# Layer 0's state space preparation moved behind the first sweep of the tokens

## The chip, the cores and the metric

The kernel runs on one core of one Trainium2 chip. A core has five engines with an instruction queue each, which they take in order: PE (TensorE, matrix multiplications; PEld is its weight load), DVE (VectorE), ACT (ScalarE), POOL (GpSimd) and SP (SyncE, which here issues most DMAs). The metric is the device time of one execution in microseconds (us). Before the change it is 5153.67 us, the median of 3 runs (5150.55 to 5157.43).

## The reference, cut to what matters

Two layers work on 2048 latent and 256 context tokens of width 1024. Each layer modulates the tokens, projects them once, feeds four mixers (A: grouped-query attention, B: differential attention, C: neighbourhood attention, D: a state space layer), gates and projects out:

```python
shift, scale, gate = jnp.split(silu(c) @ w_ada + b_ada, 3, axis=-1)
h = x * (1.0 + scale[:, None]) + shift[:, None]
(aq, ak, av, ag, ..., du, dg) = jnp.split(h @ w_in, IN_SPLITS, axis=-1)
...
yd, yd_c = s5_mixer(du, duc, a_re, a_im, log_dt, b_re, b_im, c_re, c_im, d_skip, w_glu, need_ctx)
y = jnp.concatenate([ya * silu(ag), ..., yd * silu(dg)], axis=-1) @ w_out
x_new = layer_norm(DEEPNORM_ALPHA * x + gate[:, None] * y, ln_g, ln_b)
```

Mixer D first turns its parameters into the matrices of a recurrence, and then scans the tokens in both directions. The first three lines need no token; this is what the kernel calls its preparation:

```python
lam_bar = jnp.exp(lam * dt)
b_bar = ((lam_bar - 1.0) / lam)[..., None] * b
# in s5_scan
bu = jnp.einsum('gpc,blgc->blgp', b_bar, u)
_, h = lax.associative_scan(_ssm_combine, (a, bu), axis=1)
# readout
y = einsum('gcp,blgp->blgc', c_f, h_f).real + einsum('gcp,blgp->blgc', c_b, h_b).real + d_skip * u
z = gelu(y) @ w_glu
```

## The kernel before, in words

Tokens are 18 tiles of 128 (two of context, 16 latent). Products in the projections are made in three matmuls of a high and a low part (L377 to L379). What precedes the attention of layer 0 runs in one stage, and this is its order in the code of `run`:

- **Modulation vectors** (`ada`, L242 on PE): 64 matmuls against 16 loads of `w_ada`.
- **Preparation** (`s5_prep`, L1320 to L1508): some 110 small DVE operations on 128x16 numbers, then complex products with POOL's help (`cmul`), then a loop over 16 groups. A group makes two tables, E and Fm (DVE L1479, L1481, L1483, L1485, L1487; POOL L1480, L1482), transposes E (PE L1494), multiplies Fm (PE L1501, L1502), assembles kf (ACT; DVE L1506, L1507) and stores three matrices to DRAM: `binm`, `coutm` and `t0`.
- **First sweep** (`proj_d`): for each tile, load x (L394, 512 KB), modulate (DVE L325, ACT L328), split into high and low parts (ACT L334, POOL L336, DVE L337), store them (L398, 1024 KB), 24 matmuls of 256 columns, copy (ACT L1519), transpose (PE L1523), copy out (DVE L1527). Then 16 stores of u to DRAM (L1534).
- **Group D, first pass** (L1661): loads u and `binm`, 256 matmuls, copies into B.
- **Scan** (L1578 to L1580 on DVE; carries and their products on DVE and POOL, L1624 to L1627).
- **Second sweep** (`proj("a0", ...)` with `proj_dg`): gate of D and projection of unit a0, the first half of mixer A, tile by tile from the stored parts (POOL issues these loads, L388), with an epilogue on all engines (L546 to L635). Its weights are split on POOL (L363, L367).
- **Group D, second pass** (from L1678): per group matmuls with `t0`, u, `coutm` and the states (L1701 and L1703), a GELU on ACT and DVE, a store; **third part** (L1732 to L1738): 18 tiles through `w_glu`, the last operation of each on POOL, L1737.
- **Ahead** (`F.ahead`): the first matmuls of unit b0.

All of this goes to a scheduler that simulates the engines, takes the code's order as priority and writes each engine's queue; an instruction whose operands come later may let later code pass it. Tiles of SBUF come from pools; a pool that is opened where a closed one lay makes its tiles wait for the tiles that lay there. The pool of the first sweep's loads (`h0`), that of `ada` and that of the preparation (`s5`) share one place, and group D's pool comes to lie there after them. Behind this stage `chain` gives the attention out in an order written by hand on PE, DVE and ACT; it starts with unit a0's maxima (POOL L777, PE L787). Layer 1's preparation runs beside the output projection of layer 0 and isn't touched.

Of the kernel before, what the change touches and what calls it, by code (L numbers as in the profile page):

```python
# [158 lines left out]
class Net:  # L159
# [405 lines left out]
    def slot(self, nq):  # L565
# [6 lines left out]
        return tuple(self.ub.tile([128, k, 64], F32, name=n) for k, n in ((NT, "b_v"), (nq, "b_gt")))  # L572

    def proj_a(self, l, kv, run):
        nc, io = self.nc, self.io
        nq = NT if l == 0 else NLAT
# [12 lines left out]
        def epi(ts, ps):  # L589
# [34 lines left out]
            if full:  # L624
# [10 lines left out]
            nc.scalar.activation(k2[0:64, s], tr[0:64], AF.Copy)  # L635

        return U, run(l, [(128 * kv, 128), (256 + 64 * kv, 64), (512 + 128 * kv, 128), (384 + 64 * kv, 64)], (0, 384),
                      (128, 384), epi, begin)

    def proj_b(self, l, h, run):  # L640
        nc, io = self.nc, self.io
        nq = NT if l == 0 else NLAT
# [1243 lines left out]
    def run(self):  # L1886
        self.consts()
        self.binm, self.coutm, self.t0 = {}, {}, {}
        for l in range(DEPTH):
            with ExitStack() as es:  # L1890
                side = "right" if l else "left"
                self.wp = self.pool(es, "wp", side=side)
                self.hp = self.pool(es, "hp", side=side)
                self.ep = self.pool(es, "ep", bufs=2)
                self.ub = self.pool(es, "ub")
                self.vg = [None]
                U = {}
                self.b_consts(l)

                def auto(*others):  # L1900
                    def run(l, segs, cols, ctx_cols, epi, begin):
                        begin()
                        self.sweep(l, [*others, (segs, cols, ctx_cols, epi, None, self.nc.gpsimd)])
                    return run

                def proj(u, run):
                    f = {"a": self.proj_a, "b": self.proj_b, "c": self.proj_c}[u[0]]
                    U[u], r = f(l, int(u[1]), run)
                    return r

                self.ua = self.pool(es, "ua")
                beside = lambda u: lambda F, prev: proj(u, lambda *a: self.sweep_beside(prev, F, *a))
                chunks = [(l, 4), (l, 5)] + [(l + 1, c) for c in range(4) if l + 1 < DEPTH]
                F = Fill([(u, beside(u)) for u in UNITS[1:]]
                         + [("ada", lambda F, prev: self.ada_beside(prev, F, chunks))])
                self.nd = 3
                with self.stage():
                    if l == 0:
                        with ExitStack() as es1:
                            self.ada(0, self.pool(es1, "ad"))  # L1920
                            self.s5_prep(0)
                    self.proj_d(l)
                    d = self.group_d(l)
                    next(d)
                    next(d)
                    proj("a0", auto(self.proj_dg(l)))
                    next(d, None)
                    self.ps_k = self.ps_tr
                    F.ahead(UNITS[1], AHEAD)
                self.ap = self.pool(es, "ap", bufs=2)  # L1930
                self.chain(l, F, U)
            self.nd = 2
            with self.stage():
                self.out_proj(l)
# [69 lines left out]
```

## Time and profile before

| What | us |
|---|---|
| Median of 3 runs | 5153.67 |
| The profiled execution | 5158.76 |
| Its span in the profile | 5156.9 |
| PE busy | 4681.1 (91%) |
| DVE busy | 3215.5 (62%) |
| POOL busy | 1912.5 (37%) |
| Loads of w_ada (L238), 512 KB each | 48, 4.5 to land |
| Loads of x (L394), 512 KB each | 18, 6.6 to land |

The durations in the rows below are of the one profiled execution; times of a row count from the start of its span. In the stretches, busy time counts overlapping instructions once; a busy engine is not always the one that others wait for. What ended an idle time stands behind an arrow.

### The profile page before, as it was taken

How to read it: one execution, taken by the hardware profiler on the slowest of the kernel's cores; microseconds unless marked ns; L12 is line 12 of the kernel's file. 1: busy time of each engine (PE TensorE's matmuls, PEld its weight loads, DVE VectorE, ACT ScalarE, POOL GpSimd, SP SyncE). 2: the span in 40 equal slices, each digit the busy share in tenths (PEclk: the TensorE clock that was granted, in tenths of full speed). 3: DMA queues.
4: the chain of work that ended last, by engine and by line, in shares of the span. 5: the costliest groups of instructions: out<-in, count | busy, mean ns of one | idle time of the engine just before them, and what ended most of it. 6: DMA issues, size and time to landing. Idle time of an engine off the chain costs nothing. (4 is left out here: it accounts for less than half of the span.)

```text
span 5156.9 us, 85866 instructions
## 1 busy us (share of the span) xinstructions
PE 4681.1 (91%) x31076; PEld 3585.3 (70%) x31076; DVE 3215.5 (62%) x7061; ACT 2568.4 (50%) x6522; POOL 1912.5 (37%) x3035
## 2 busy tenths in 40 slices
PE   7788998899999999998996879988999999999998
PEld 3686646665678777776676866566657777877777
DVE  8473767676674846724972737686767648476245
ACT  3332346634675856744341233466346658566431
POOL 4363443434233233321642534434342332333112
PEclk8899999999999999999998999999999999999999
DMA  7847212322235344253668573123223343433432
GB/s 255 287 151 202 88 41 66 98 95 72 91 121 167 103 144 132 83 178 116 194 213 281 169 198 109 49 65 98 95 72 98 111 152 100 155 122 117 130 134 107
DMA packets 360184, 677.66 MB, mean 131 GB/s; under 512 B 161872, under 2 KB 262224, under 8 KB 306768
## 3 DMA queue, kind: packets, MB, share of 16 engines
q0 software_dynamic: 54432, 396.39, 22.9%
q1 hardware_dynamic: 299280, 270.47, 17.9%
q10 hardware_dynamic: 6048, 5.31, 0.3%
q8 instruction: 247, 4.05, 0.3%
q14 instruction: 177, 1.45, 0.1%
HBM read 561.66 MB, written 110.36 MB: 130 GB/s over the span
## 5 line engine op out<-in xcount | busy, mean ns | idle before, releaser
L377 PE MATMUL pj<-WH,hs 128*128 128x256 f32 (+2 forms) x2592 | 814.9, 314 | 22.1 <-ACT b_v L733 7.1
L378 PE MATMUL pj<-WL,hs 128*128 128x256 f32 (+2 forms) x2592 | 753.3, 291 | 2.7 <-POOL WL L367 2.7
L379 PE MATMUL pj<-WH,hs 128*128 128x256 f32 (+2 forms) x2592 | 752.3, 290 | 0.0
L1114 ACT ACTIVATE PT<-tr 128x512 f32<-128x512 f32 (+1 forms) x788 | 440.5, 559 | 310.0 <-PE tr L1100 303.3
L377 PEld LDWEIGHTS pj<-WH,hs 128*128 128x128 f32 x2592 | 498.1, 192 | 125.3 <-issue 68.2
L388 POOL DMA_DIRECT2D hs<-hs x378 | 227.7, 603 | 956.0 <-PE pj L379 475.6
L378 PEld LDWEIGHTS pj<-WL,hs 128*128 128x128 f32 x2592 | 499.2, 193 | 26.6 <-POOL WL L367 3.3
L881 ACT ACTIVATE PT<-sx 128x512 f32<-128x512 f32 x584 | 315.3, 592 | 378.1 <-PE sx L879 367.6
L379 PEld LDWEIGHTS pj<-WH,hs 128*128 128x128 f32 x2592 | 497.7, 192 | 2.4 <-issue 2.4
L1045 DVE TENSOR_REDUCE sm<-sx 128x1 f32<-128x1024 f32 (+1 forms) x276 | 321.8, 1166 | 210.2 <-PE sx L1001 208.9
L1060 ACT ACTIVATE Ta<-sx,sm 128x1024 f32<-128x1024 f32 (+1 forms) x340 | 324.5, 955 | 108.2 <-DVE sm L1054 87.2
L886 PE MATMUL acc<-PT,a_v 128*64 128x512 f32 (+1 forms) x1168 | 315.8, 617 | 0.0
L897 POOL TENSOR_TENSOR Ta<-Ta,PT 128x512 f32<-128x512 f32 x160 | 219.5, 1389 | 204.4 <-ACT PT L881 203.9
L1126 PE MATMUL acc<-PT,b_v 128*64 128x128 f32 (+1 forms) x3200 | 277.9, 290 | 4.4 <-DVE sm L1073 1.5
L1001 PE MATMUL sx<-b_kst,qs 128*128 128x512 f32 (+2 forms) x618 | 218.3, 441 | 58.1 <-ACT Ta L1060 57.4
L814 DVE TENSOR_REDUCE mxa<-sy 128x1 f32<-128x1024 f32 (+1 forms) x256 | 209.8, 820 | 89.9 <-PE sy L812 86.8
L897 DVE TENSOR_TENSOR Ta<-Ta,PT 128x512 f32<-128x512 f32 x288 | 217.0, 794 | 77.0 <-ACT PT L881 76.5
L878 PE MATMUL sx<-Tb,a_kst 128*128 128x512 f32 x584 | 246.8, 423 | 19.5 <-ACT PT L881 19.5
L1100 PE MATMUL tr<-ident,Ta 128*128 128x128 f32 x1576 | 246.5, 278 | 13.9 <-ACT PT L1114 10.2
L1045 DVE TENSOR_REDUCE sm<-sy 128x1 f32<-128x768 f32 (+1 forms) x260 | 245.4, 944 | 15.7 <-PE sy L1001 14.4
L814 DVE TENSOR_REDUCE mxa<-sz 128x1 f32<-128x512 f32 x256 | 175.5, 686 | 123.5 <-PE sz L812 121.7
L377 PE MATMUL s<-WH,hs 128*128 128x256 f32 (+1 forms) x576 | 193.4, 337 | 44.9 <-DMA hs<-hs 20.7
(388 smaller groups left out, 12175.2 us busy)
## 6 DMA issues: line engine op xcount, KB each, us to landing
hs<-hs POOLq DMA_DIRECT2D x378, 1024.0 KB, 5.2
hs<-hs SPq DMA_DIRECT2D x36, 1024.0 KB, 4.8
hs<-in_w_ada SPq DMA_DIRECT2D x48, 512.0 KB, 4.5
wst<-in_w_in SPq DMA_DIRECT2D x576, 32.0 KB, 1.9
yin<-y SPq DMA_DIRECT2D x30, 512.0 KB, 4.0
h<-in_xT SPq DMA_DIRECT2D x18, 512.0 KB, 6.6
U<-ud SPq DMA_DIRECT2D x64, 144.0 KB, 3.6
x<-zn SPq DMA_DIRECT2D x18, 512.0 KB, 2.7
```

The costliest lines, as they stand in the source:

```text
L377: nc.tensor.matmul(ps, H[:, k, :], WH[k][:, c0:c1], start=(k == 0), stop=False)
L378: nc.tensor.matmul(ps, H[:, k, :], WL[k][:, c0:c1], start=False, stop=False)
L379: nc.tensor.matmul(ps, L[:, k, :], WH[k][:, c0:c1], start=False, stop=(k == NK - 1))
L814: nc.vector.tensor_reduce(nm if one else mx[:, j:j + 1], s, axis=AX.X, op=OP.max, negate=one)
L878: nc.tensor.matmul(o[:, h * 512:h * 512 + w], kst[:, ks], Q[0][:, h, :w], start=True, stop=False)
L881: nc.scalar.activation(PTs[x][h][:, :w], o[:, h * 512:h * 512 + w], AF.Exp, scale=0.125)
L886: nc.tensor.matmul(acc[h * 64:(h + 1) * 64, :w], v[:, kts[x], :], PT[h][:, :w], start=(x == 0), stop=(x == n - 1))
L897: eng.tensor_tensor(sums[e][:, h, :w], first[:, :w], PT[h][:, :w], op=OP.add)
L1045: nc.vector.tensor_reduce(mx[:, j:j + 1] if len(tiles) > 1 else nm, s, axis=AX.X, op=OP.max, negate=len(tiles) == 1)
L1060: nc.scalar.activation(r["P"](a, b), src, AF.Exp, bias=r["sm"][:, 5:6], accum_out=r["sm"][:, 6 + j:7 + j])
L1114: nc.scalar.activation(PT[:w, x:y], tr[:w, x * 128:y * 128].rearrange("p (a b) -> p a b", b=128), AF.Copy)
L1126: nc.tensor.matmul(acc[t][half * 64:half * 64 + 64, :], G["v"][:w, kt, :], PT[:w, j, :], start=(x < 2), stop=x >= nkt - 2)
```

## The change

The call `self.s5_prep(0)` moves from ahead of `self.proj_d(l)` to behind it. The code of the preparation is the same, and so is its work.

```diff
                     if l == 0:
                         with ExitStack() as es1:
                             self.ada(0, self.pool(es1, "ad"))
-                            self.s5_prep(0)
                     self.proj_d(l)
+                    if l == 0:
+                        self.s5_prep(0)
                     d = self.group_d(l)
```

With the call, the scheduler's queues change. On DVE, around the first tiles of the first sweep, the preparation (L1479 to L1507) and the modulation (L325) stood mixed before:

```order
L325 TENSOR_SCALAR h_1280<-h_1280,mod_78 128x128
L1507 TENSOR_TENSOR kf<-d,kf 16x16
L325 TENSOR_SCALAR h_1280<-h_1280,mod_78 128x128 x3
L1479 TENSOR_TENSOR m_763<-s_44_523,s_4_346 128x288
L1481 TENSOR_TENSOR m_765<-s_44_523,s_4_346 128x288
L1479 TENSOR_TENSOR m_796<-s_43_522,s_42_471 128x256
L1481 TENSOR_TENSOR m_798<-s_43_522,s_42_471 128x256
L1506 TENSOR_TENSOR kf<-d,s_45_534 16x16
```

At the same place there is now the sweep alone (L1527 copies its transposed result out):

```order
L325 TENSOR_SCALAR h_389<-h_389,mod_78 128x128 x4
L325 TENSOR_SCALAR h_431<-h_431,mod_78 128x128 x4
L337 TENSOR_TENSOR hs<-h_389,hs 128x768
L337 TENSOR_TENSOR hs<-h_431,hs 128x768
L325 TENSOR_SCALAR h_478<-h_478,mod_78 128x128 x4
L1527 COPY a_kst<-pj 128x16x8
L1527 COPY a_k_337<-pj 128x16x8
```

All 276 instructions of the preparation that stood ahead of or in the first sweep on DVE now stand behind its last split (L337). There they are mixed with the second sweep's epilogue (L546, L609, L627, L628 and others), here in the loop over the groups:

```order
L627 CAST ks<-kf 128x64
L546 SCALAR_TENSOR_TENSOR ks<-gth,s 128x256
L1507 TENSOR_TENSOR kf<-d,kf 16x16
L1483 TENSOR_TENSOR E<-m_1800,m_1801 128x256
L1487 TENSOR_TENSOR E<-m_1802,m_1803 128x256
L1479 TENSOR_TENSOR m_1810<-s_44_1441,s_4_1264 128x288
L1481 TENSOR_TENSOR m_1812<-s_44_1441,s_4_1264 128x288
L628 TENSOR_TENSOR ks<-kf,ks 128x64
```

Nine of the second sweep's 18 tiles have their epilogue (by L609) inside the preparation's queue; before, none had. On ACT, the copies L1678 that open group D's second pass stood among the second sweep's epilogue:

```order
L634 ACTIVATE a_kst<-pj 128x128
L635 ACTIVATE a_k_2928<-pj 64x128
L598 ACTIVATE pe<-s 128x320
L599 ACTIVATE a_v<-s 128x64
L1678 ACTIVATE big_2587<-big_2148 64x2304 x2
L602 ACTIVATE sq<-pe 128x192
```

Now the second sweep's epilogue ends before them, and the first tiles of unit b0 (L659, L660) stand between the scan's last carry (L1611) and the copies:

```order
L634 ACTIVATE a_kst<-pj 128x128
L635 ACTIVATE a_k_2928<-pj 64x128
L1611 ACTIVATE scan_c<-big_2429 128x2x16 x7
L659 ACTIVATE pe<-pj 128x2x64
L660 ACTIVATE pe<-pj 128x2x128
L537 ACTIVATE gth<-pe 128x128
L1678 ACTIVATE big_2587<-big_2148 64x2304 x2
```

What moved in between is the whole rest of the second sweep: it is done ahead of the copies now, where before it ran on behind them. POOL's last two products of the scan (L1626, L1627) stand behind a step of b0's epilogue (L541) in the same way.

## Rows read from the trace of the kernel before

**Rows 1.** Stretches: us, busy us (count) of PE, PEld, DVE, ACT, POOL; clock, DMA, GB/s.

```profile
62.00:155.00 93.00, 75.24 (x417) 51.76 (x416) 78.98 (x192) 45.06 (x104) 52.70 (x54) 0.85 0.88 286
155.00:207.00 52.00, 39.84 (x241) 37.02 (x241) 28.76 (x87) 23.75 (x48) 18.17 (x17) 0.80 0.84 294
207.00:272.00 65.00, 45.88 (x405) 42.18 (x406) 22.10 (x86) 16.98 (x51) 16.91 (x29) 0.87 0.83 248
272.00:363.00 91.00, 78.52 (x505) 76.87 (x504) 79.23 (x147) 25.40 (x93) 64.84 (x73) 0.92 0.44 142
363.00:437.00 74.00, 65.05 (x457) 62.26 (x456) 31.67 (x82) 32.17 (x66) 18.37 (x29) 0.98 0.81 213
437.00:491.00 54.00, 40.49 (x135) 21.57 (x133) 13.74 (x31) 9.36 (x30) 30.96 (x51) 0.89 0.64 180
```

**Rows 2.** Timeline: start us, us, engine, line, operation [idle before <-releaser].

```profile
490.18 0.72 POOL L1737 TENSOR_TENSOR yth<-yth,U 128x256 f32<-128x256 f32 x1 [0.60 <-DMA U<-dg]
...
490.98 2.33 POOL L777 TENSOR_TENSOR qn<-a_q,one 128x256 fp32r<-128x256 f32 x4
...
491.64 0.69 PE L787 MATMUL tr<-ident,qn 128*128 128x128 f32 x2 [6.90 <-POOL qn L777]
```

**Rows 3.** Four lines: ns min/median/max, first and last start us, forms.

```profile
L242 PE MATMUL pj<-hs,cs x64: 591/592/1057, 10.6 to 51.7; 128*2 128x512 f32 x64
L1507 DVE TENSOR_TENSOR kf<-d,kf x16: 152/155/163, 56.4 to 154.7; 16x16 f32<-16x16 f32 x16
L1519 ACT ACTIVATE ks<-s x18: 357/384/386, 77.4 to 201.5; 128x256 f32<-128x256 f32 x18
L1527 DVE COPY a_k<-pj x18: 269/279/282, 85.4 to 207.2; 128x128 f32<-128x128 f32 x18
```

**Rows 4.** Timeline of ACT, line 1519: two of eight such rows.

```profile
163.79 0.39 ACT L1519 ACTIVATE ks<-s 128x256 f32<-128x256 f32 x1 [2.88 <-PE s L379]
...
201.46 0.39 ACT L1519 ACTIVATE ks<-s 128x256 f32<-128x256 f32 x1 [3.11 <-PE s L379]
```

**Rows 5.** Waits from 155 to 205 us: engine, waited for, us, times, longest.

```profile
ACT h L328 <- DMA h<-in_xT: 8.9, 7, 2.6
```

**Rows 6.** Timeline, the preparation with no sweep beside it.

```profile
13.32 0.17 DVE L1420 TENSOR_TENSOR s<-s 128x16 f32<-128x16 f32 x1 [3.76 <-DMA s<-in_s_a]
...
28.39 0.42 DVE L1435 TENSOR_TENSOR cm<-s,s 128x256 f32<-128x256 f32 x1
...
43.50 0.88 PE L1494 MATMUL d<-ident,E 128*128 128x128 f32 x4
...
66.56 1.12 PE L1494 MATMUL d<-ident,E 128*128 128x128 f32 x4 [0.23 <-DVE kf L1507]
```

**Rows 7.** Groups by form, 13 to 62 us: busy us, mean ns, idle before.

```profile
L1479 DVE TENSOR_TENSOR m<-s,s 128x256 f32<-128x256 f32 x5 | 4.1, 814 | 0.0
```

**Rows 8.** Timeline of SP, POOL and PE behind the first sweep.

```profile
207.28 7.13 SPq L1534 DMA_DIRECT2D ud<-a_kst  x8
...
224.59 5.52 PE L1661 MATMUL d<-U,bm 128*64 128x144 f32 x48 [9.45 <-DMA U<-ud]
...
227.33 0.50 POOL L363 CAST WH<-wst 128x384 fp32r<-128x384 f32 x1 [22.76 <-DMA wst<-in_w_in]
```

**Rows 9.** Timeline of POOL in the scan, the first and last of its eight products.

```profile
322.20 2.40 POOL L1624 TENSOR_TENSOR big<-y,scan_c 128x1024 f32<-128x1024 f32 x1 [2.24 <-ACT scan_c L1611]
...
360.57 2.40 POOL L1627 TENSOR_TENSOR big<-big,big 128x1024 f32<-128x1024 f32 x1
```

**Rows 10.** Groups of DVE from 272 to 363 us: busy us, mean ns, idle.

```profile
L1580 DVE TENSOR_TENSOR big<-big 128x576 f32<-128x576 f32 (+1 forms) x24 | 17.4, 725 | 1.7 <-DVE big L1579 0.5
L1578 DVE TENSOR_TENSOR big<-coef,big 128x576 f32<-128x576 f32 x15 | 12.4, 829 | 0.4
L1579 DVE TENSOR_TENSOR big<-big,big 128x288 f32<-128x288 f32 x16 | 8.2, 514 | 0.2
```

**Rows 11.** DMA queues, 363 to 437 us: packets, MB, share of 16 engines (q0: L388).

```profile
q0 software_dynamic: 576, 4.19, 18.2%
```

## The prediction

> **What bounds the kernel now.** I read the stretches of layer 0 first, then backwards from the place where the attention starts. That place is the hand-over at 491 us: POOL ends the last L1737 of group D's third part, goes straight on to L777, the first operation of unit a0's maxima, and PE, idle for 6.9 us, is released by it [rows 2]. So the attention waits for the end of group D, and from there on the order is written by hand and the same in both kernels. What counts is how long it takes until group D is done. Its chain is a row of steps, and the stretches are cut where one ends [rows 1]: modulation vectors to 52.3 us (the last matmul of L242 starts at 51.7 and takes 0.6) [rows 3], first sweep to 207.5 (the last copy L1527 starts at 207.2), first pass to 272, scan to 363, second pass to 437, third part to 491.
>
> In which of these does the preparation cost anything? Its loop runs beside the sweep: L1507, once in a group, goes from 56.4 to 154.7 us [rows 3]. DVE is busy 79 of the 93 us of that stretch, and only 29 of the 52 behind it [rows 1]. The sweep itself went at (201.5 - 77.4)/17 = 7.3 us a tile over its whole length by L1519 [rows 3], but at (201.46 - 163.79)/7 = 5.38 us once the preparation had ended [rows 4]. There ACT waits for the loads of x [rows 5] while 294 GB/s move [rows 1]: a tile loads 512 KB and stores 1024, 1.57 MB, which at that rate takes 5.3 us. So that late pace is set by memory traffic, and the reader is to see two things: the preparation slows the sweep, and it is itself nearly free in the stretch ahead of 66 us and half free beside a sweep that waits for memory.
>
> **The change part by part.** Nothing is removed or added; the same instructions and DMAs run. The sum goes step by step along the chain to the hand-over, each with its value and both its ends.
>
> *First sweep, shorter.* Its modulation no longer queues behind the preparation. A load to its L1519 takes about two paces (two buffers of x), so the first one comes at 52.3 + 1.5 (copy, transpose, bias) + 2 x 5.4 = 64.6 instead of 77.4. Seventeen paces of 5.38 and 3 for the last transposes and copies: 64.6 + 91.5 + 3 = 159 us, against 207.5. Ends 153 and 165, since the stretches show 286 and 294 GB/s and no faster sweep. Gain 48 us.
>
> *The preparation's front, now on the path.* From its first operation to the first transposes it took 43.5 - 13.3 = 30.2 us with hardly anything beside it [rows 6]. Now POOL has ten splits of the second sweep's weights ahead of its first complex product, and these begin 20 us behind the first sweep (227.3 against 207.5), since their loads queue on SP behind the 16 stores of u that begin at 207.3 [rows 8]. I take 35, ends 30 and 42. The five loads of the preparation are issued on SP ahead of those stores, so they add nothing.
>
> *The loop over 16 groups.* With nothing beside it, four groups took 66.56 - 43.50 = 23.1 us, 5.8 each [rows 6]; beside the first sweep, (154.7 - 56.4)/15 = 6.55 each [rows 3]. The queue has nine tiles of the second sweep's epilogue in it, where the first sweep gave eleven or so, but each with six operations on POOL instead of one. I take 6.8: 109 us, ends 93 (5.8) and 128 (8.0). Its 48 stores and 192 matmuls ride along; PE does the second sweep's matmuls in between, and that cover holds.
>
> *First pass.* Before, it began 17 us behind the sweep, waiting for u (9.45 us on PE) [rows 8]. That wait falls away, as u is in DRAM long before. But `binm` of the last group must go to DRAM and back, and the pass then reloads u and `binm` through two buffers as before: 47 us as in 224.6 to 272; ends 38 (no waiting) and 65 (the whole stretch).
>
> *Scan.* Of 91 us, DVE's recurrence takes 17.4 + 12.4 + 8.2 = 38 [rows 10], and POOL's eight products of 2.4 us, 19, end at 363 [rows 9]; both ran mixed with the second sweep. About six of its tiles stay in the scan, none of them at its end, but there POOL now waits for b0's first two tiles before its last two products, and the copies L1678 queue on ACT behind the same tiles. I take 80; ends 57 (the two sums) and 91.
>
> *Second pass.* 74 us at 213 GB/s, DMA 81% busy [rows 1]: 15.8 MB, of which 4.2 are POOL's loads for the sweeps' tiles [rows 11], which don't run beside it any more. If memory sets it, the rest takes 74 x 11.6/15.8 = 54; if its own chain of matmul, square, tanh and product does, 74. I take 62.
>
> *Third part.* 54 us, as before: 18 tiles, each with a load and a store, and little was beside it.
>
> Sum: 159 + 35 + 109 = 303 us for the end of the preparation, + 47 = 350, + 80 = 430, + 62 = 492, + 54 = 546, against 491. The change costs 55 us. Of it, 144 us of preparation come onto the path; 48 come back from the sweep, 17 from the wait for u and its neighbourhood, and 23 from the scan and the second pass, which lose the second sweep beside them (the borders of the stretches are whole us). The profiled execution took 5158.8 (span 5156.9 and 1.9 around it), 5.1 above the median; I add the 55 to the median: 5153.7 + 55 = 5209 us. In the back of layer 0 and in layer 1 some rows change places with their neighbours; I put that at nothing, give or take 5.
>
> At the loop a rule of the Trainium skill speaks against the change. First the rows: a DVE product of two 128x256 operands takes 0.42 us while POOL rests [rows 6] and 0.81 in the loop beside POOL's products [rows 7]. The rule (the Trainium skill, SBUF — State Buffer, "Who interferes with whom"): a DVE instruction with two SBUF inputs and a GpSimd one that reads SBUF exclude each other, and the later one waits for all of the other. The trace agrees that the operation is doubled. By the rule the epilogue's DVE and POOL work would add up instead of overlapping; by the loop's row beside the first sweep, 6.55, they overlap for the most part. The second rival below is the rule's case; its price is worked out from rows there.
>
> **The rivals.**
>
> *Faster.* The second sweep is used up beside the preparation, and what follows runs alone at its floors: scan and second pass at 57 + 54 = 111 instead of 142 (-31), loop at 5.8 (-16), front at 30 (-5), first pass at 38 (-9). 546 - 31 - 16 - 5 - 9 = 485, and with the first sweep too at its end of 153, 479, 12 us earlier than before: 5142. It decides from the point where these savings come to over 55 us. For it: DVE is idle for 43 of 65 and 42 of 74 us in the two passes [rows 1]. Against it: the loop beside a sweep has its own row, and the order puts b0's tiles ahead of the second pass.
>
> *DVE and POOL exclude each other in the loop.* Then the preparation's 5.8 us and the epilogue's share add up: 9/16 of a tile, whose POOL work I bound by half of the 64.8 us that POOL is busy in the scan's stretch for ten tiles [rows 1], some 3.2 us a tile, so 1.8, and as much for DVE's part at most: 5.8 + 3.6 = 9.4, and 9.4 against 6.8 is 42 us more: 5251. Against it stands the 6.55.
>
> *No change.* The attention starts when unit a0 is ready, whatever group D does, or the delay is taken up in the 4600 us behind it: 5154. For it: POOL's order is the scheduler's, not written by hand. Against it: in the new order too all 18 of L1737 stand ahead of L777, and PE is 91% busy with a fixed order behind.
>
> That the preparation slips back beside the first sweep can't be: all of it stands behind the last split on DVE.
>
> **How the numbers follow.** Forecast 0.72, the exclusion 0.11, no change 0.09, faster 0.08. The half ranges of the terms (6, 6, 17, 13, 17, 10) give 31 us as the root of the sum of squares, so the forecast's own range is 5178 to 5240. For 8 in 10 over all cases I take 5162 to 5246, which lets the low side reach towards no change and the high side towards the exclusion. About 0.2%, 10 us, is what a measurement of this kernel tells from no change. Slower by more than that: the forecast nearly whole (0.71) and the exclusion (0.11), 0.82. Within: 0.01 of the forecast, the case of no change and a part of the faster case, 0.11. Faster: 0.07.
>
> **What would show it.** In the changed profile L1527 ends near 159 us, at 5.4 us a tile by L1519; the first L1494 near 194; L1507 ends near 303; L1661 runs to 350; L1678 starts near 430; the last L1737 ends near 546 and L777 follows it at once. From there to the end the time is as before. It is wrong if L777 starts near 491 or earlier, if the loop takes over 8 or under 6 us a group, or if the time behind the hand-over differs by more than 10 us.

## The result, and the profile after

The changed kernel takes 5224.18 us (median of 4 runs, 5219.71 to 5227.45), the kernel before beside it 5152.11 (4 runs, 5144.89 to 5157.43): a ratio of 1.0128, 95% interval 1.011 to 1.0147. It is slower by 72 us; the forecast was 5209, 55 slower than the median known then (5153.67). The profiled executions differ by 65.1 us in span (5222.0 and 5156.9).

The hand-over first. In the timeline of the changed kernel POOL ends group D's last product and goes on to the attention's first operation at 547.7 us. PE, idle for some 5 us, takes it up at once. This answers to [rows 2], and it is 56.7 us later; the forecast had 546, 55 later.

```profile
546.93 0.72 POOL L1737 TENSOR_TENSOR yth<-yth,U 128x256 f32<-128x256 f32 x1 [0.82 <-DMA U<-dg]
...
547.73 2.32 POOL L777 TENSOR_TENSOR qn<-a_q,one 128x256 fp32r<-128x256 f32 x4
548.39 0.29 PEld L787 LDWEIGHTS tr<-ident,qn 128*128 128x128 f32 x2 [5.96 <-POOL qn L777]
```

The chain in front of it, by source lines of the changed kernel (duration in ns as minimum, median, maximum, then the first and last start in us). The first five lines answer to [rows 3, 6].

```profile
L242 PE MATMUL pj<-hs,cs x64: 591/592/1062, 10.6 to 52.6; 128*2 128x512 f32 x64
L1519 ACT ACTIVATE ks<-s x18: 357/383/387, 67.3 to 159.9; 128x256 f32<-128x256 f32 x18
L1527 DVE COPY a_k<-pj x18: 280/281/283, 71.1 to 162.4; 128x128 f32<-128x128 f32 x18
L1494 PE MATMUL d<-ident,E x64: 271/273/421, 202.9 to 300.7; 128*128 128x128 f32 x64
L1507 DVE TENSOR_TENSOR kf<-d,kf x16: 153/154/163, 212.0 to 306.4; 16x16 f32<-16x16 f32 x16
L1661 PE MATMUL d<-U,bm x256: 285/286/338, 317.9 to 357.0; 128*64 128x144 f32 x128
L1678 ACT ACTIVATE big<-big x2: 4114/4122/4129, 442.8 to 446.8; 64x2304 f32<-64x2304 f32 x2
L1710 DVE SCALAR_TENSOR_TENSOR y<-yth,d x16: 447/454/456, 455.6 to 502.5; 128x288 f32<-128x288 f32 x16
L1737 POOL TENSOR_TENSOR yth<-yth,U x18: 722/725/729, 515.1 to 546.9; 128x256 f32<-128x256 f32 x18
```

The sweep ends 45 us earlier than before (162.7 with the copy's 0.28, against 207.5) and goes at (159.9 - 67.3)/17 = 5.45 us a tile instead of 7.3. The preparation, whose last L1507 started at 154.7 before, now begins behind the sweep, and its last L1507 starts at 306.4. The stretches of the changed kernel, cut at these ends (us, then busy us and count of PE, PEld, DVE, ACT and POOL, the granted clock, the DMA share, GB/s), answer to [rows 1]:

```profile
62.00:163.00 101.00, 79.94 (x492) 72.97 (x493) 44.64 (x121) 48.98 (x99) 30.71 (x26) 0.83 0.80 287
163.00:203.00 40.00, 21.92 (x117) 19.31 (x115) 28.15 (x124) 2.92 (x11) 17.91 (x32) 0.79 0.69 201
203.00:255.00 52.00, 44.96 (x240) 30.20 (x241) 50.78 (x114) 16.40 (x48) 46.54 (x59) 0.90 0.73 214
255.00:307.00 52.00, 48.06 (x254) 32.73 (x253) 32.56 (x89) 15.66 (x47) 39.76 (x50) 0.93 0.66 185
307.00:359.00 52.00, 49.23 (x468) 45.13 (x467) 27.37 (x123) 18.94 (x63) 16.37 (x29) 1.00 0.83 261
359.00:443.00 84.00, 46.09 (x295) 44.45 (x294) 79.25 (x125) 19.10 (x70) 63.13 (x69) 0.77 0.43 137
443.00:503.00 60.00, 40.52 (x260) 38.49 (x261) 23.79 (x53) 25.11 (x36) 0.00 (x0) 0.81 0.70 178
503.00:548.00 45.00, 35.37 (x72) 14.51 (x70) 9.68 (x19) 6.90 (x18) 13.31 (x19) 0.88 0.40 110
```

The reader is to see two things. The front (163 to 203) and the loop (203 to 307) are stretches of their own now, and DVE, busy 50.8 of 52 us in the loop's first half, is the fullest engine there; in the second half that is PE, busy 48.1 us, with the second sweep's matmuls beside the loop's, while DVE is busy 32.6. In the last two stretches POOL is busy 0 and 13.3 us, where it was 18.4 and 31.0 before: the second sweep is over by then. Of its 18 tiles eight have their L609 by the end of the loop (not nine, as the queue was read ahead of the prediction), four more start it in the first pass and the last six in the scan, the last at 398.9 us, where before the last one started at 437.8. So the second pass and the third part have less beside them.

### The profile page after: what moved, and what is told of

Its sections match the earlier page's. It is cut to its first block, busy times and chain, and to the rows that moved or that the text cites. A ratio compares the mean times of both kernels' runs of the same rounds, so it can differ in the third digit from the quotient of the medians.

```text
span 5222.0 us, 85852 instructions
## 1 busy us (share of the span) xinstructions
PE 4697.5 (90%) x31076; PEld 3588.8 (69%) x31076; DVE 3231.4 (62%) x7061; ACT 2568.9 (49%) x6522; POOL 1922.6 (37%) x3035
## 3 DMA queue, kind: packets, MB, share of 16 engines
q0 software_dynamic: 54432, 396.39, 22.6%
## 5 line engine op out<-in xcount | busy, mean ns | idle before, releaser
L1114 ACT ACTIVATE PT<-tr 128x512 f32<-128x512 f32 (+1 forms) x788 | 440.2, 559 | 306.4 <-PE tr L1100 301.8
L388 POOL DMA_DIRECT2D hs<-hs x378 | 226.3, 599 | 920.9 <-PE pj L379 455.2
L1045 DVE TENSOR_REDUCE sm<-sx 128x1 f32<-128x1024 f32 (+1 forms) x276 | 321.8, 1166 | 212.0 <-PE sx L1001 211.1
```

The costliest lines, as they stand in the source:

```text
L1045: nc.vector.tensor_reduce(mx[:, j:j + 1] if len(tiles) > 1 else nm, s, axis=AX.X, op=OP.max, negate=len(tiles) == 1)
L1114: nc.scalar.activation(PT[:w, x:y], tr[:w, x * 128:y * 128].rearrange("p (a b) -> p a b", b=128), AF.Copy)
```

## The experiments

Theory A: the 57 us at the hand-over are the preparation, put as one serial step on group D's chain, less what the first sweep and the later stages get back; it stands there because its tiles get the place in SBUF that the first sweep's buffers leave. Rivals: the later call itself costs, by the scheduler's ranks (B); or it is the mixing with the second sweep, or memory traffic.

### The same call, another place in SBUF

```diff
-            p = self.pool(es, "s5")
+            p = self.pool(es, "s5", side="left" if l else "right")
```

The edit is made first in the changed kernel and later, as a control, in the kernel before.

> The changed kernel with one word more: layer 0's preparation takes its tiles from the other side of SBUF, where no pool of the first sweep lies. The call stays behind the sweep in the code. In the order that comes out, the preparation stands mixed with the modulation and the first sweep again. Theory A (the 57 us come from the preparation's tiles lying in the place that the sweep's tiles have to give free, so that it stands behind the sweep as one serial step): L1507 ends near 155 us as in the kernel before and not near 306, the first sweep ends near 207 and not 163, L777 starts near 491 (485 to 500), the time is 5152, give or take 10. Rival B (the later call is what costs, by the rank that the scheduler gives to work that comes later in the code, in layer 0's stage or in layer 1's): L777 starts over 515 us, the time is 5190 to 5230.

> The kernel before with only the other change of the first experiment in it: layer 0's preparation takes its tiles from SBUF's other side. Theory A: the place costs nothing by itself, L777 near 491 to 497, time 5152 to 5177. If it is near 5177 like the first experiment, the 18 us that that one lies above the kernel before are the place's; if near 5152, they belong to the later call.

Measured: the changed kernel with the other place 5177.29 us, ratio to the kernel before 1.0033 (1.0021 to 1.0046); the kernel before with the other place 5158.63, ratio 1.0007 (0.9997 to 1.0016). By source lines, first the changed kernel with the other place, then the control:

```profile
L1507 DVE TENSOR_TENSOR kf<-d,kf x16: 152/155/163, 55.8 to 165.9; 16x16 f32<-16x16 f32 x16
...
L777 POOL TENSOR_TENSOR qn<-a_q,one x14: 604/615/627, 496.9 to 616.1; 128x256 fp32r<-128x256 f32 x14
```

```profile
L1507 DVE TENSOR_TENSOR kf<-d,kf x16: 151/155/163, 56.8 to 156.4; 16x16 f32<-16x16 f32 x16
...
L777 POOL TENSOR_TENSOR qn<-a_q,one x14: 602/612/625, 494.4 to 612.9; 128x256 fp32r<-128x256 f32 x14
```

With the call still behind the sweep the preparation runs beside the sweep again, and the hand-over is 50.8 us earlier than in the changed kernel (496.9 and 547.7). So the place in SBUF decides, as A has it. The time of 5177 misses A's 5152, give or take 10, and B's 5190 to 5230 alike. Against the control, which has the place but not the later call, 2.5 us stand at the hand-over and 12.2 behind it (span less hand-over: 5177.3 - 496.9 = 4680.4, against 5162.6 - 494.4 = 4668.2). By the medians the control takes as long as the kernel before, and the first kernel 0.33%, some 18 us, longer. By what was expected of the control these 18 us belong to the later call: a small share for B. Whether it is the call's rank or what any newly drawn order can bring (below) isn't separated.

### The preparation as a serial step ahead of the sweep

```diff
                         with ExitStack() as es1:
                             self.ada(0, self.pool(es1, "ad"))
-                            self.s5_prep(0)
+                        self.s5_prep(0)
                     self.proj_d(l)
```

> The kernel before, with the call of layer 0's preparation still ahead of the first sweep but outside the block that holds the pool of the modulation vectors: now the sweep's tiles must wait for the place of the preparation, and on DVE all of the preparation stands ahead of the sweep. Theory A (the cost is what of the preparation is left without cover): the front (13 to 43 us) and some three groups of the loop lie beside the modulation vectors; the loop ends near 43.5 + 16 x 5.8 = 136 us, the sweep then needs 12 us for its first tile and 94 for the rest (pace 5.4) and ends near 243, and the tail of the kernel before (491 - 207 = 284 us) brings L777 to about 527; time 5152 + 36 = 5188, 5175 to 5205. Rival (what costs in the changed kernel is that the preparation is mixed with the second sweep, not that it is serial): the tail is untouched here, so the time is within 15 us of 5152. Rival (a preparation on the path costs the same whichever side of the sweep it stands on): 5210 to 5235.

Measured: 5233.38 us, ratio 1.0138 (1.0122 to 1.0153), the hand-over at 552.2. By source lines of this kernel:

```profile
L1420 DVE TENSOR_TENSOR s<-s x1: 175/175/175, 55.2 to 55.2; 128x16 f32<-128x16 f32 x1
L1494 PE MATMUL d<-ident,E x64: 273/421/477, 79.0 to 155.6; 128*128 128x128 f32 x64
L1507 DVE TENSOR_TENSOR kf<-d,kf x16: 154/155/164, 89.8 to 158.7; 16x16 f32<-16x16 f32 x16
...
L1527 DVE COPY a_k<-pj x18: 275/280/281, 179.0 to 273.0; 128x128 f32<-128x128 f32 x18
```

The expected 5188 was wrong: the preparation starts at 55.2, behind the modulation vectors, and not at 13, so nothing of it is covered. Its call now stands behind the close of the modulation vectors' pool, whose place its tiles take; its loads are issued from 53.46 on, after the last L242. The time lies where the third case was priced (5210 to 5235): a preparation on the path costs the same on either side of the sweep. As a serial step it takes 104 us; the sweep ends at 273.3, 111 later than in the changed kernel, and the tail of 279 us is that of before (283.5). The cost of +61 us at the hand-over comes from a serial preparation with nothing mixed into its neighbours. The rival in which the mixing is what costs falls, since here it is absent and the price is the same. In the changed kernel the mixing stretches the preparation from 104 to 144 us, and what follows the preparation takes 241 us (547.7 - 306.6) instead of 283.5, so there it nearly pays for itself. This also gives the preparation's own lengths with nothing beside it: front 79.0 - 55.2 = 23.8 us, loop (158.7 - 89.8)/15 = 4.6 us a group.

### What is the loop worth, beside the sweep and behind it?

Eight of the 16 groups left out, first the work alone (each result stored twice), then work and stores; in both kernels. In the first pair:

```diff
-            for g in range(NG):
+            half = l == 0
+            for g in range(NG // 2 if half else NG):
...
-                nc.sync.dma_start(self.binm[l][g], ...)
+                for j in (g, g + 8) if half else (g,):
+                    nc.sync.dma_start(self.binm[l][j], ...)
```

and so for `coutm` and `t0`. In the second pair only the loop's bound is halved, and the passes read with `g % 8` in layer 0. Between the two the stores were left out with all of the work kept (`if l > 0 or g < 2:` ahead of each of the three).

> The kernel before, with the same eight groups of layer 0's loop left out and all 48 stores kept. Theory A (beside the first sweep the loop is partly free: it slows the sweep from 5.4 to 8.6 us a tile as long as it runs): the loop ends near 93 us, two tiles go at 8.6 and sixteen at 5.4, the sweep ends near 185 instead of 207, time 5152 - 22 = 5130 (5122 to 5140), so that the same omission is worth less than half of what it is worth in the changed kernel. Rival (a group costs as much beside the first sweep as behind it): 5152 - 48 = 5104. Rival (beside the sweep the loop is wholly free): 5152, give or take 6.

> The changed kernel, with layer 0's loop over 16 groups computing only eight of them and storing each result twice: the group tables of the other eight are left out, the 48 stores all run. Theory A (the loop is wholly on the path behind the sweep, at 6.3 us a group): L1507 ends near 256 instead of 306, L777 starts 45 to 50 us earlier, near 500, time 5224 - 48 = 5176 (5168 to 5186). Rival (memory traffic of the second sweep or the stores set that stretch, and the loop is beside it): less than 20 us earlier, time over 5200.

> The kernel before, with layer 0's loop computing all 16 groups but storing only the first two: 42 of its 48 stores (14 x 704 KB = 10.1 MB) are left out, and the passes read the tables of those two groups for all. Theory C, formed on the halved loop, which stored as many bytes as the full one and moved the end of the sweep by nothing: beside the first sweep the preparation costs its memory traffic. The sweep's stretch moves at 286 to 294 GB/s, so 10.1 MB less are 35 us: the sweep ends near 172 us instead of 207, L777 starts near 456, time 5152 - 35 = 5117 (5108 to 5130). Rival (DVE's work for the loop slows the sweep, as the prediction took it): the sweep ends at 200 or later, time over 5143.

> The kernel before, with eight of the 16 groups of layer 0's loop left out, work and stores; the passes read the first eight groups' tables twice. Theory D (beside the first sweep the preparation meets two limits that lie close together, engine work in order on DVE and memory traffic, so that taking away half of one alone gives nothing): with both halved the sweep loses half of its 48 us, ends near 183 (178 to 192), L777 starts near 467, time 5152 - 24 = 5128 (5118 to 5140). Rival (something third holds the sweep, such as the order of its first tiles behind the modulation): the sweep ends at 203 or later, time over 5143.

> The changed kernel with the same eight groups left out, work and stores. Theory A (the loop is on the path): it ends 8 x 6.3 = 50 us earlier, near 256; from the runs with the loop's stores kept and with the front taken out, of 42 us that come off the preparation 23 to 26 reach the hand-over, because the second sweep's work then lies beside the passes: L777 25 to 40 us earlier, 508 to 523, time 5224 - 25 to 40 = 5184 to 5199. Rival (the stores' traffic set that stretch): over 45 us earlier, under 5180.

Measured, with the ratio to the kernel before and the start of L777:

| kernel | us | ratio (95%) | sweep ends | L777 | L777 against its own kernel |
|---|---|---|---|---|---|
| before, half the work | 5159.31 | 0.9998 (0.9987 to 1.0009) | 207.3 | 489.1 | -1.9 |
| before, stores out | 5169.96 | 1.0018 (1.0006 to 1.003) | 203.7 | 486.0 | -5.0 |
| before, half of both | 5126.46 | 0.9944 (0.9925 to 0.9962) | 181.9 | 464.9 | -26.1 |
| after, half the work | 5190.84 | 1.0058 (1.0041 to 1.0075) | 163.4 | 522.3 | -25.4 |
| after, half of both | 5189.15 | 1.0064 (1.0046 to 1.0083) | 167.1 | 512.8 | -34.9 |

In the kernel before, half of the loop's work gives nothing, where theory A expected 22 us, and leaving out 10.1 MB of its 11.5 MB of stores ends the sweep 3.8 us earlier, where theory C expected 35, and gives nothing in the time. Half of both gives 26 us, within 2 us of what theory D expected at the sweep's end (183). The stretches of the three kernels from 62 to 125 us show why: half the work, then the stores out, then half of both.

```profile
62.00:105.00 43.00, 30.38 (x138) 19.47 (x136) 23.66 (x60) 14.56 (x34) 15.29 (x15) 0.73 0.99 291
105.00:125.00 20.00, 9.95 (x45) 8.92 (x46) 5.88 (x17) 6.83 (x14) 2.99 (x2) 0.59 0.97 299
```

```profile
62.00:105.00 43.00, 35.52 (x160) 22.22 (x157) 35.53 (x87) 19.79 (x45) 28.22 (x29) 0.63 0.49 168
105.00:125.00 20.00, 16.81 (x113) 11.86 (x113) 20.00 (x49) 11.12 (x25) 13.60 (x16) 1.00 0.64 214
```

```profile
62.00:105.00 43.00, 35.43 (x182) 24.68 (x182) 29.42 (x79) 22.42 (x51) 16.82 (x17) 0.74 0.92 304
105.00:125.00 20.00, 14.68 (x92) 12.71 (x92) 9.40 (x26) 10.71 (x22) 5.99 (x4) 0.89 0.80 270
```

With half the work DVE is busy 23.7 of 43 us, and the DMA engines are nearly full (0.99 and 0.97). With the stores out the DMA share falls to 0.49 and 0.64, and DVE is busy 35.5 of 43 us and then all of the time (20.00 of 20). So beside the first sweep the preparation stands against two limits that lie close together, the engines' queues, DVE's above all, and memory traffic. The scheduler drew up a new order for each of these kernels, so the exact shares are not separated, but relieving either limit alone gives back next to nothing of the 45 us that the sweep lost.

In the changed kernel the loop's end moves by 41 us (306.4 to 265.7) and by 48 (to 258.6), and the hand-over by 25 and 35. The loop is on the path there, as A has it, but not at full price: the time of half the work, 5191, lies above A's 5168 to 5186. With half of both, 5189 lies in the range expected of it (5184 to 5199); leaving out the stores too brings the hand-over 9.5 us further forward (522.3 and 512.8). The rival in which traffic alone sets that stretch wanted under 5180.

### The front taken off the path

```diff
-            p = self.pool(es, "s5")
+            p = self.pool(es, "s5", side="left" if l else "right")
...
+            yield
+            if l == 0:
+                p = self.pool(es, "s5l")
             for g in range(NG):
```

The part up to `yield` is called ahead of `proj_d(0)`, the rest behind it.

> The changed kernel, with the preparation cut in two: its front (up to the loop) is called ahead of the sweep with its tiles on SBUF's other side, the loop over 16 groups behind the sweep as in the changed kernel. Theory A (front and loop are both on the path there, one behind the other): the front lies beside the modulation vectors for nothing, the first sweep still ends near 163 us, the loop starts at once and ends near 163 + 16 x 6.3 = 264 instead of 306. L777 starts 40 us earlier, near 508, if everything behind moves along; with only the 26 of 41 us that the halved loop gave back, near 521. Time 5184 to 5198. Rival (the loop waits for the second sweep's weights or traffic and not for the front): the loop ends at 290 or later, time over 5210.

Measured: 5203.05 us, ratio 1.0086 (1.0071 to 1.0102). By source lines (L1497 is L1494 of the other kernels, L1510 is L1507):

```profile
L1497 PE MATMUL d<-ident,E x64: 270/274/477, 161.3 to 259.2; 128*128 128x128 f32 x64
L1510 DVE TENSOR_TENSOR kf<-d,kf x16: 154/155/165, 168.3 to 264.1; 16x16 f32<-16x16 f32 x16
...
L777 POOL TENSOR_TENSOR qn<-a_q,one x12: 607/614/626, 525.1 to 604.4; 128x256 fp32r<-128x256 f32 x12
```

The loop ends at 264.1, as expected, 42 us earlier than in the changed kernel; the hand-over comes 22.6 earlier, near the lower of the two expectations (26), and the time lies 5 us above the expected 5184 to 5198. The other 20 us go to the stages behind: less of the second sweep is done by the end of the loop (four of its tiles by L609, against eight). Here L1661 runs from 276.0 to 322.0 (46 us, against 39 in the changed kernel), and L1710 from 427.1 to 481.0 (54, against 47). Beside these last 54 us POOL's queue still loads 2.10 MB; in the changed kernel it loads nothing beside the same lines, and in the kernel before 4.19 MB in the second pass [rows 11], where these lines took 56.7 us.

### Fewer bytes for the same tables

An attempt at a kernel faster than both: `t0` is stored as the rows that it is cut from.

```diff
-        self.t0[l] = dr.tile([NG, 128, 384], F32, name=f"t0_{l}")
+        self.t0[l] = dr.tile([NG, 16, 496], F32, name=f"t0_{l}")
...
-                    t2 = load("t0", self.t0[l][g:g + 2].rearrange("g p n -> p g n"), 384)
+                    t2 = p.tile([128, 2, 384], F32, name="t0")
+                    for j in range(2):
+                        k0 = self.t0[l][g + j]
+                        nc.sync.dma_start(t2[:, j], bass.AP(tensor=k0.tensor, offset=k0.offset,
+                                                            ap=[[16, 8], [496, 16], [1, 384]]))
```

> The kernel before, with the Toeplitz tables t0 of both layers stored as the 16x496 rows that they are cut from (31 KB a group instead of 192), and spread over 128 partitions only when the second pass loads them (two DMAs of 192 KB instead of one of 384). Theory C (traffic beside the first sweep is what the preparation costs): 16 x 161 KB = 2.6 MB less, 9 us at 290 GB/s; the sweep ends near 198, L777 starts near 482, time 5143 (5136 to 5150); a little more if layer 1's stores cost anything. Rival (traffic isn't it, or the second pass loses on its two loads what the sweep wins): 5152, give or take 6.

Measured: 5194.85 us, ratio 1.0068 (1.0054 to 1.0082), slower than the kernel before. In this kernel (L1714 is L1710):

```profile
L1527 DVE COPY a_k<-pj x18: 269/280/283, 87.5 to 205.5; 128x128 f32<-128x128 f32 x18
L1714 DVE SCALAR_TENSOR_TENSOR y<-yth,d x16: 440/455/456, 373.5 to 439.3; 128x288 f32<-128x288 f32 x16
```

The sweep wins 1.7 us, not 9, as the two limits have it. The second pass takes 65.8 us between its first and last L1710, where the kernel before took 56.7 (379.6 to 436.3); in layer 1 the last L1678 and the last L1710 start 79.1 us apart instead of 61.3. At the hand-over of layer 0 this kernel is only 2.9 us late (493.9), so most of what it loses lies behind it. Whether it is the two loads in place of one or their source of overlapping rows wasn't separated. No version here that does all of the work beats the kernel before.

## Why the prediction was right, point by point

The direction, the place in the kernel and the mechanism were right: the attention waits for group D, the preparation moves onto that chain, the sweep gives about a third of it back (45 of 144 us). Stage by stage:

| step | forecast us | measured | from |
|---|---|---|---|
| sweep's end | 159 | 162.7 | last L1527 |
| front | 35 | 40.2 | to the first L1494 at 202.9 |
| loop | 109 | 103.7 | last L1507 ends 306.6 |
| first pass | 47 | 53 | to 359.5, as before 2.5 behind the last L1661 |
| scan | 80 | 83 | to the first L1678 at 442.8 |
| second pass | 62 | 60 | last L1710 ends 503.0 |
| third part | 54 | 45 | L777 at 547.7 |

*Sweep.* The pace was right (5.38 forecast, 5.45 measured), but its reason only in half. The prediction read the slow sweep of before as the preparation's work on DVE slowing a sweep that waits for memory late. The runs show two limits at once, and the 48 stores, which it let "ride along" with the loop, fill the memory traffic beside the sweep.

*Front.* Sized 5 us short. What it has beside it is the second sweep's start: from 163 to 203 us POOL waits 20.0 us for the weights of L363, the splits lie between the preparation's products, and DVE waits 4.6 us for POOL's (L1436). The preparation's five loads were put at nothing; DVE waits 3.3 us for one of them (L1364 for `in_s_dt`). With nothing beside it the front took 23.8 in the serial experiment.

*Loop.* 6.29 us a group ((306.4 - 212.0)/15), between the lower end and the value taken. The lower end of 5.8 was no floor: 4.6 in the serial experiment. The rival in which DVE and POOL exclude each other wanted 9.4 and falls as it was priced: in the loop's first half DVE's 50.78 us and POOL's 46.54 lie in the same 52. By the rule of the Trainium skill (SBUF — State Buffer, "Who interferes with whom") the two wait for each other. The trace of the serial kernel agrees:

```profile
88.44 3.07 POOL L1480 TENSOR_TENSOR m<-s,s 128x256 f32<-128x256 f32 x1 [1.43 <-DVE kf L1506]
89.44 0.40 DVE L1479 TENSOR_TENSOR m<-s,s 128x256 f32<-128x256 f32 x1
...
93.75 0.82 POOL L1480 TENSOR_TENSOR m<-s,s 128x256 f32<-128x256 f32 x1
93.99 0.86 DVE L1481 TENSOR_TENSOR m<-s,s 128x256 f32<-128x256 f32 x1
```

From 88.44 to 91.51 one POOL product lies beside a row of DVE's, which take 0.40 to 0.44 each; right behind it, where the two alternate, DVE's take 0.83 to 0.92. So part of both busy times is waiting, and they can't be added up. How much of the loop that waiting costs stays open, as no run here takes POOL's products away.

*First pass.* The 47 were the matmuls' own stretch of before; added to it are 11.3 us from the end of L1507 to the first L1661. They are not a way to DRAM and back for the last group's `binm`, as the prediction has it, but the first loads of the pass, which are issued right behind the preparation's last store:

```profile
306.63 0.32 SPq L1508 DMA_DIRECT2D t<-kf  x1
307.05 1.68 SPq L1649 DMA_DIRECT2D U<-ud  x2
308.82 0.44 SPq L1643 DMA_DIRECT2D bm<-binm  x1
...
317.87 3.25 PE L1661 MATMUL d<-U,bm 128*64 128x144 f32 x48 [0.79 <-DMA bm<-binm]
```

The load at 308.82 is that of groups 0 and 1. PE does the second sweep's matmuls meanwhile and is idle for 0.79 us only. The matmuls of the pass then ran in 39 us instead of 45, with PE's granted clock at 1.00 (its upper level, 2.4 GHz) in that stretch; before, PE had been idle for 9.45 us ahead of them [rows 8], and the mean clock of the stretch was 0.87 [rows 1]. Of the 11.3 us some 6 come back so, and the step takes 53 for 47.

*Second pass and third part.* With the second sweep gone from beside them, the second pass took 14 us less (74 to 60), 12 forecast, and the third part 9 less (54 to 45), none forecast. "Little was beside it" was wrong there: POOL's busy time fell from 31.0 to 13.3 us and the traffic from 180 to 110 GB/s [rows 1].

*Behind the hand-over.* Put at nothing, give or take 5; measured 8.4 (4674.3 against 4665.9 us from L777 to the span's end). It left its own range, within the 10 us that the prediction allowed. It isn't shown to come from the change: in the other kernels in which nothing but layer 0's preparation is changed, this stretch lies between 4657 (half the work, after) and 4682 (front taken off), and the control, the kernel before with only the place in SBUF changed, has 4668. The kernel before itself took from 5145 to 5171 us in the 15 runs beside the first experiments. The difference is of the size that a newly drawn order, or one run against another, brings; its cause stays open.

The sum to the hand-over was off by 2 us, with errors of 2 to 9 in its terms that cancel, so that it came so close is in part luck. The 72 us between the medians are 56.7 at the hand-over, 8.4 behind it, and 7.0 that the two profiled executions lie nearer to each other than their medians (the one of before 6.6 above its median, the one of after 0.4 below). Of the rivals, "faster" fails at its first point: the second sweep isn't used up beside the preparation, where only eight of 18 tiles are done, and the scan and the second pass saved some 21 us together (272 to 437 before, 359.5 to 503 after), where that case needed 54 (165 to 111). "No change" fails at L777.

## What to carry to other kernels

A step that is moved in the code lands where its tiles find their place in memory: when the queues are drawn up under waits for tiles, look first at whose place the moved step takes. Work beside a stage that waits is not free by the share of one engine; halve its work and its traffic separately and together before calling either the limit. And what comes off a serial step reaches the end only in part (here 23 of 42, 25 of 41 and 35 of 48 us) as long as other work, the second sweep here, has to be done in the same stretch.

## What the runs showed of the hardware beyond that

Ten megabytes of stores fewer did not speed the loop that issues them: 6.53 us a group without them ((155.2 - 57.3)/15) and 6.55 with them. With nothing beside it but its own stores it took 4.6, so it is what runs beside it that costs a group 1.7 to 2 us, beside the first sweep and the second alike; whether by its work on the engines or by its own traffic isn't separated. Twice the stores to a group, in the two kernels with half the work, did slow it: to 7.3 us beside the first sweep ((105.2 - 54.4)/7) and 7.6 behind it ((265.7 - 212.4)/7), where eight groups with their own stores alone took 5.3 ((93.5 - 56.5)/7) and 6.1 ((258.6 - 216.2)/7).
